# A hybrid streaming-encoder layer: the first receptance tile projected from the unscaled input, the output's row tiles finished one by one

## The chip, the cores and the metric

One core of a Trainium2 chip runs the whole kernel. The metric is the device time of one execution in microseconds (us), the median of several runs.

## The reference

One layer on a sequence of 512 tokens with 1024 channels, all in float32. `rms_norm`, one wide projection, three token mixers side by side (a short gated convolution, an RG-LRU, an RWKV-7 time mix with a state of 64 x 64 per head), a gated merge, an output projection with a residual, then a squared-ReLU MLP with a residual, and a last `rms_norm`.

```python
h = rms_norm(x, norm1_g[l])
p = h @ w_in[l]                       # 12 wide pieces, r, k, v among them
pc = token_shift(pc, rwkv_mu[l])      # p + (previous token's p - p) * mu
r, k, v, xw, xa, xg = _split(pc, ...)
...
y = rwkv7_recurrence(r, decay, k, v, kk, a)   # in chunks of 64 tokens
...
x = x + m @ w_out[l]
x = x + jnp.square(jax.nn.relu(h2 @ mlp_w1[l])) @ mlp_w2[l]
return rms_norm(x, final_g)
```

`rms_norm` divides by the root of the mean square over the channels and multiplies by a gain. The division is one number per token, so `h @ w` can be had as `(x * gain) @ w`, divided afterwards.

## The kernel before

Activations lie transposed in SBUF: channels on the 128 partitions (8 slices, `KT`), the 512 tokens along the free axis. Each float32 matrix product is made of three matmuls of a fast kind (`mm3`, lines 163 to 165): every operand is split in a high part (`whi`, `hh`) and the rest (`wlo`, `hl`). One projection tile of 128 output channels is 24 matmuls of 128x128 by 512 columns in one PSUM bank. Its weights come by one DMA on SP's queue (`raw`, two buffers); ScalarE casts the high part (`whi`, line 142) and VectorE subtracts for the low part (`wlo`, line 99), three buffers each.

In the prologue, the unscaled input times the gain is split into `xgh`, `xgl`; the first projections (`lr0`, `lr1`, and `k0`) are made of these (`proj_raw`), while the sum of squares and its inverse root `rsb` are worked out. Their results are then multiplied by `rsb` (`unscaled`) and mixed with the token before (`shift`: one ScalarE and one VectorE instruction). `pro_scale` makes `hh`, `hl` for all other projections: a multiply by `rsb` (five slices on GpSimd, three on VectorE), a ScalarE product, a VectorE difference (`hl`).

Behind it, four groups of heads run. For each, `krv` projects k, r and v of the group's channel tiles (`k0`, `r0`, `k1`, `r1`, `v0`, `v1` in group 0) and makes decay and key terms; `amat` makes the matrices `pA` of every chunk, masked into `AXt` on VectorE; `inverse` inverts a triangular matrix per chunk by substitution on VectorE (`Z`, `dg`), put together by small matmuls `pG`, `pT`; `chain` walks the chunks. `ab` is filler for TensorE: it projects the other branches (`xb`, `gb`, `gatb`, `c`, `x`, `b`, `ga`) of two channel tiles a group (tile 6 first in group 0). `weave` alternates between the critical generator and the filler; the priorities given there, and the numbers of buffers, decide the order in which each engine's instructions stand. Each engine then runs its own row strictly in that order and waits for others by semaphores.

The tail is the end of the MLP's second product. The result lies by tokens: four row tiles of 128 tokens (`i`), two halves of 512 channels each (`h`), eight PSUM banks `acc`. For the last two of 32 contraction slices, the function `last` issues the six matmuls that each half still lacks, then adds the residual, sums the squares (ScalarE, `fss`), takes the root (`fsd`), multiplies by the final gain `fgt` and scales by the inverse root. It is a generator, called in the order 0, 1, 2, 0, 1, 3, 3, 2, so that the second parts of tiles stand behind the first parts of later ones.

Of the kernel before, what the change touches and what calls it, by code (L numbers as in the profile page):

```python
# [93 lines left out]
def block_kernel(ctx, tc, xt, win, par, mulr, sw, wout, w1, w2, fg, cst, eyes, out):  # L94
# [176 lines left out]
    def proj_raw(w, t):  # L271
        for kt in range(KT):
            mm3(t, *wslice(w, kt), xgh(kt), xgl[:, kt], start=kt == 0, stop=kt == KT - 1)
# [21 lines left out]
    def shift(pt, mu, omu, o):  # L295
        ac.activation(o, pt, AF.Copy, scale=omu)
        stt(o[:, 1:], pt[:, 0:S - 1], mu, o[:, 1:], MUL, ADD)
# [32 lines left out]
    shift(unscaled(t_lr0, "us0"), mul[:, 0:1], omul[:, 0:1], lr)  # L330
    t_k0 = pp.tile([P, S], F32, tag="pp", name="pp")
    proj_raw(load_w(win[CN[("k", 0)]]), t_k0)
    ac.activation(lr[0:64], lr[0:64], AF.Tanh)
    lws = sp.tile([P, S], F32R, name="lws")
    las = sp.tile([P, S], F32R, name="las")
# [10 lines left out]
    lgh, lgl = split(sp, lg, "lg")  # L346
    k0 = WP("ks")
    shift(unscaled(t_k0, "us0"), pv("mu_k", 0), dvp(OMK, 0), k0)
    pro_ctx.close()


# [33 lines left out]
    def krv(g, G_):  # L385
        G_.AR = pk.tile([P, 2, NC, 2, L], F32, tag="AR", name="AR")
        G_.BK = pk.tile([P, 2, NC, 2, L], F32, tag="BK", name="BK")
        G_.pl = sp.tile([P, 2, NC], F32, tag="pl", name="pl", bufs=2)
        G_.v = [sp.tile([P, S], F32, tag=f"v{h}", name=f"v{h}", bufs=2) for h in range(2)]
        G_.bv = [sp.tile([P, S], F32, tag=f"bv{h}", name=f"bv{h}", bufs=2) for h in range(2)]  # L390
        for jj in range(2):
            j = 2 * g + jj
            rs = WP("rs")
            if j == 0:
                ks = k0
            else:
                ks = WP("ks")
                t = yield from proj(("k", j))
                shift(t, pv("mu_k", j), dvp(OMK, j), ks)
            sq = WP("a1")  # L400
            ac.activation(sq, ks, AF.Square, scale=pv("kk", j))
            sqh, sql = split(pk, sq, "b")
            pn = pm.tile([P, S], F32, tag="pm", name="pn")
            pe.matmul(pn, bd, sqh, start=True, stop=False)
            pe.matmul(pn, bd, sql, start=False, stop=True)
            kk = WP("a5")
            rsqrt_rows(pk, kk, pn, 1e-24)
            stt(kk, ks, pv("kk", j), kk, MUL, MUL)
            yield
            t = yield from proj(("r", j))  # L410
            shift(t, pv("mu_r", j), dvp(OMR, j), rs)
            yield
            swh, swl = load_sw(pk, "swa", j, 0, 2)
            pw = pm.tile([P, S], F32, tag="pm", name="pw")
            pe.matmul(pw, swh[:, 0], lws, start=True, stop=False)
            pe.matmul(pw, swl[:, 0], lws, start=False, stop=True)
            sig = WP("a1")
            ac.activation(sig, pw, AF.Tanh, bias=pv("w0", j), scale=0.5)
            v.tensor_scalar(out=sig, in0=sig, scalar1=1.0, scalar2=None, op0=ADD)
            pa = pm.tile([P, S], F32, tag="pm", name="pa")  # L420
            pe.matmul(pa, swh[:, 1], las, start=True, stop=False)
            pe.matmul(pa, swl[:, 1], las, start=False, stop=True)
            av = WP("a4")
            ac.activation(av, pa, AF.Tanh, bias=pv("a0", j), scale=0.5)
            cum = WP("a2")
            v.tensor_tensor_scan(out=cum, data0=smk, data1=sig, initial=0.0, op0=MUL, op1=ADD)
            PP = pk.tile([P, NC, L + 1], F32, tag="PPt", name="PPt")
            gp.memset(PP[:, :, 0:1], 1.0)
            Pt = PP[:, :, 1:L + 1]
            ac.activation(Pt, c3(cum), AF.Exp, scale=-0.5 * CW)  # L430
            v.tensor_copy(G_.pl[:, jj], PP[:, :, L])
            pinv = WP("a3")
            ac.activation(pinv, cum, AF.Exp, scale=0.5 * CW)
            stt(G_.AR[:, jj, :, 0], c3(kk), -1.0, PP[:, :, 0:L], MUL, MUL)
            tt(G_.AR[:, jj, :, 1], c3(rs), Pt, MUL)
            t_ = WP("a1")
            stt(t_, av, 1.0, kk, ADD, MUL)
            stt(G_.BK[:, jj, :, 0], c3(t_), 0.5, c3(pinv), MUL, MUL)
            kp = WP("a2")
            ts2(kp, av, pv("ka", j), dvp(OKA, j), MUL, ADD)  # L440
            tt(kp, kp, ks, MUL)
            tt(G_.BK[:, jj, :, 1], c3(kp), c3(pinv), MUL)

            if jj == 0:
                rk = [WP(f"rk{h}") for h in range(2)]
            for h in range(2):
                r = slice(64 * h, 64 * h + 64)
                stt(rk[h][64 * jj:64 * jj + 64], rs[r], part[r, PI["rk"], j:j + 1], kp[r], MUL, MUL)
        rk = [split(pk, rk[h], ("a1", "a3") if h else "b") for h in range(2)]
        for h in range(2):  # L450
            q = 2 * g + h
            t = yield from proj(("v", q))
            shift(t, pv("mu_v", q), dvp(OMV, q), G_.v[h])
            yield
        for h in range(2):
            pb = pm.tile([P, S], F32, tag="pm", name="pb")
            for i in range(2):
                pe.matmul(pb, bd, rk[h][i], start=i == 0, stop=i == 1)
            tt(G_.bv[h], pb, G_.v[h], MUL)
# [449 lines left out]
    with tc.tile_pool(name="mw", bufs=2) as mw, \  # L909
# [41 lines left out]
        with tc.tile_pool(name="fin", bufs=1, side="right") as fin:  # L951
# [19 lines left out]
                        mlp2(fi, w, i, h)  # L971
            wl2 = [load_w(w2[fi]) for fi in range(NF - 2, NF)]
            def last(i):
                ss = fin.tile([P, 2], F32, tag="fss", name="fss", bufs=2)
                x3f = xr[:, i] if i < 3 else fin.tile([P, D], F32, name="x3f")
                for h in range(2):
                    hs = slice(h * S, (h + 1) * S)
                    for d_ in range(2):
# [1 line left out]
                    stt(xr[:, i, hs], acc[i][h], sc2[:, i:i + 1], xr[:, i, hs], MUL, ADD)  # L980
                    junk = fin.tile([P, S], F32, tag="fj", name="fj", bufs=2)
                    ac.activation(junk, xr[:, i, hs], AF.Square, accum_out=ss[:, h:h + 1])
                    (v if (i, h) == (3, 0) else gp).tensor_tensor(out=x3f[:, hs], in0=xr[:, i, hs], in1=fgt[:, hs], op=MUL)
                sd = fin.tile([P, 2], F32, tag="fsd", name="fsd", bufs=2)
                tt(sd[:, 0:1], ss[:, 0:1], ss[:, 1:2], ADD)
                ac.activation(sd[:, 1:2], sd[:, 0:1], AF.Sqrt, bias=epst[:, 0:1], scale=1.0 / D)
                v.reciprocal(sd[:, 0:1], sd[:, 1:2])
                yield
                for h in range(2):
                    hs = slice(h * S, (h + 1) * S)  # L990
                    if h == 0 and i != 2:
                        ac.activation(x3f[:, hs], x3f[:, hs], AF.Copy, scale=sd[:, 0:1])
                    else:
                        v.tensor_scalar(out=x3f[:, hs], in0=x3f[:, hs], scalar1=sd[:, 0:1], scalar2=None, op0=MUL)
                    (ac if h == 0 and i != 2 else sy).dma_start(out[i, :, hs], x3f[:, hs])

            gens = [last(i) for i in range(4)]
            for i in (0, 1, 2, 0, 1, 3, 3, 2):
                next(gens[i], None)
        ps.close()  # L1000


# [72 lines left out]
```

## Time and profile before

| | us |
|---|---|
| median of 3 runs | 1125.88 |
| lowest, highest | 1125.72, 1127.33 |
| the profiled execution's own time | 1126.26 |
| its span, first to last instruction | 1124.5 |

The span is one execution as the profiler saw it; its own time is 1.76 us longer. A row of a timeline says when an instruction started, how long it took, its engine and line, what it wrote and read, and in brackets how long the engine was idle before it, and what ended that. PE is TensorE's matmul, DVE is VectorE, ACT ScalarE, POOL GpSimd, SP the queue that issues the weights' DMAs. "x2" is a run of like instructions in one row.

### The profile page before, as it was taken

The page shows a single profiled execution, that of the slowest core. Times are in us where ns is not written, and L with a number is a line of the kernel's source. Part 1 is how long each engine was busy: PE and PEld are TensorE (multiplying, and loading weights), DVE is VectorE, ACT ScalarE, POOL GpSimd, SP SyncE. Part 2 cuts the span into 40 slices and gives each one's busy share as a digit, 9 for nine tenths or more (in the row PEclk, how much of TensorE's full clock was granted, in tenths as well). Part 3 has the DMA queues.
Part 4 walks back from the last instruction along what each step waited for, and adds up shares of the span by engine and source line. Part 5 has one row for each costly group of instructions (what it writes and reads, how often), then busy time and mean ns, then how long its engine had stood idle before and what let it go on. Part 6 is the DMA issues. An engine that isn't in the chain of part 4 may idle for free.

```text
span 1124.5 us, 16256 instructions
## 1 busy us (share of the span) xinstructions
PE 1087.3 (97%) x6396; PEld 869.7 (77%) x6396; DVE 766.3 (68%) x1369; ACT 519.2 (46%) x837; POOL 58.9 (5%) x99
## 2 busy tenths in 40 slices
PE   8899989999989999989999989999999999999996
PEld 5677867778867678867678867898888888888885
DVE  7998995989986889975888967686444443222224
ACT  6655355534457534456534474564344333112113
POOL 2200000000000000000000020100000000000003
PEclk8999997999999999999999999999999999999998
DMA  6232222231233131232231262455322225322222
GB/s 212 71 103 80 73 74 77 62 103 57 90 117 99 58 103 57 89 120 88 61 95 65 85 206 85 171 180 161 109 95 94 94 94 191 105 98 94 93 94 75
DMA packets 37772, 114.60 MB, mean 102 GB/s; under 512 B 4544, under 2 KB 8128, under 8 KB 37696
## 3 DMA queue, kind: packets, MB, share of 16 engines
q1 hardware_dynamic: 30768, 95.48, 26.6%
q0 software_dynamic: 6352, 17.30, 4.5%
q8 instruction: 50, 0.82, 0.3%
q10 hardware_dynamic: 576, 0.79, 0.2%
q14 instruction: 26, 0.21, 0.1%
HBM read 104.64 MB, written 8.91 MB: 101 GB/s over the span
## 4 chain that ended last, share of the span: by engine, by line
PE 71%; DVE 22%; issue 3%; ACT 2%; DMA 1%; SPq 0%; ACTq 0%; DVEq 0%
PE pp L163 8%; PE pp L164 8%; PE pp L165 8%; PE acc L165 6%; PE acc L164 6%; PE acc L163 6%; PE p L164 5%; PE p L165 5%; PE p L163 5%; DVE wlo L99 5%; DVE dg L99 4%; DVE Z L99 3%; PE pA L471 2%; DVE u L102 2%; PE py L578 2%
## 5 line engine op out<-in xcount | busy, mean ns | idle before, releaser
L99 DVE TENSOR_TENSOR wlo<-raw,whi 128x1024 fp32r<-128x1024 f32 (+1 forms) x172 | 209.4, 1218 | 215.7 <-ACT whi L142 213.6
L142 ACT CAST whi<-raw 128x1024 fp32r<-128x1024 f32 (+1 forms) x172 | 178.1, 1036 | 286.1 <-PE acc L165 125.7
L165 PE MATMUL pp<-hh,wlo 128*128 128x512 f32 x696 | 278.0, 401 | 5.8 <-DVE wlo L99 5.8
L164 PE MATMUL pp<-hl,whi 128*128 128x512 f32 x696 | 278.3, 400 | 3.9 <-DVE hl L102 3.9
L163 PE MATMUL pp<-hh,whi 128*128 128x512 f32 x696 | 278.5, 401 | 1.4 <-DVE ks L102 0.6
L165 PEld LDWEIGHTS pp<-hh,wlo 128*128 128x128 f32 x696 | 131.9, 190 | 34.4 <-DVE wlo L99 7.3
L163 PEld LDWEIGHTS pp<-hh,whi 128*128 128x128 f32 x696 | 132.0, 190 | 31.9 <-ACT u L664 2.1
L164 PEld LDWEIGHTS pp<-hl,whi 128*128 128x128 f32 x696 | 132.0, 190 | 31.6 <-DVE hl L102 4.7
L165 PE MATMUL p<-h2h,wlo 128*128 128x512 f32 (+1 forms) x264 | 101.2, 383 | 0.0
L163 PE MATMUL p<-h2h,whi 128*128 128x512 f32 (+1 forms) x264 | 101.1, 383 | 0.0
L164 PE MATMUL p<-h2l,whi 128*128 128x512 f32 (+1 forms) x264 | 101.0, 383 | 0.0
L163 PE MATMUL acc<-whi,ah 128*128 128x512 f32 x256 | 99.6, 389 | 0.0
L164 PE MATMUL acc<-wlo,ah 128*128 128x512 f32 x256 | 99.6, 389 | 0.0
L165 PE MATMUL acc<-whi,al 128*128 128x512 f32 x256 | 99.6, 389 | 0.0
L165 PEld LDWEIGHTS p<-h2h,wlo 128*128 128x128 f32 x264 | 49.6, 188 | 9.7
L163 PEld LDWEIGHTS p<-h2h,whi 128*128 128x128 f32 x264 | 49.6, 188 | 9.7
L164 PEld LDWEIGHTS p<-h2l,whi 128*128 128x128 f32 x264 | 49.6, 188 | 9.5
L165 PEld LDWEIGHTS acc<-whi,al 128*128 128x128 f32 x256 | 48.0, 188 | 10.1
L164 PEld LDWEIGHTS acc<-wlo,ah 128*128 128x128 f32 x256 | 48.0, 188 | 10.1
L163 PEld LDWEIGHTS acc<-whi,ah 128*128 128x128 f32 x256 | 48.0, 188 | 9.8
L99 DVE TENSOR_TENSOR Z<-Z,dg 64x31 f32<-64x31 f32 (+15 forms) x124 | 42.2, 340 | 4.1
L99 DVE TENSOR_TENSOR dg<-Z 64x31 f32<-64x31 f32 (+15 forms) x124 | 42.2, 340 | 4.1
(299 smaller groups left out, 1533.8 us busy)
## 6 DMA issues: line engine op xcount, KB each, us to landing
raw<-in_win SPq DMA_DIRECT2D x88, 512.0 KB, 3.5
raw<-in_w SPq DMA_DIRECT2D x64, 512.0 KB, 3.5
raw<-in_wout SPq DMA_DIRECT2D x16, 512.0 KB, 3.5
swr<-in_sw SPq DMA_DIRECT2D x16, 128.0 KB, 2.1
x2T<-in_xt POOLq DMA_DIRECT2D x4, 512.0 KB, 7.1
x2d<-st POOLq DMA_DIRECT2D x8, 256.0 KB, 2.6
xr<-x2d POOLq DMA_DIRECT2D x1, 2048.0 KB, 9.1
xT<-in_xt SPq DMA_DIRECT2D x3, 512.0 KB, 6.7
```

What stands on the lines that cost most here:

```text
L99: return v.tensor_tensor(out=o, in0=a, in1=b, op=op)
L102: return v.scalar_tensor_tensor(out=o, in0=a, scalar=s, in1=b, op0=op0, op1=op1)
L142: ac.copy(hi[:, sl], raw[:, sl])
L163: pe.matmul(ps, wh, xh, start=start, stop=False)
L164: pe.matmul(ps, wh, xl, start=False, stop=False)
L165: pe.matmul(ps, wl, xh, start=False, stop=stop)
L471: pe.matmul(pts[h][:, ci], G_.BK[rows, jj, c], G_.AR[rows, jj, c], start=True, stop=True)
L578: mm = pe.matmul(py[64 * h:64 * h + 64, jj], w, x, start=first and jj == 0, stop=last, skip_group_check=True)
```

## The change

There are two parts. In the prologue the projection of `r0` is made by `proj_raw` from the unscaled input, into the PSUM bank of the pool's tag `pS` (which the state products use later), and is multiplied by `rsb` before its `shift`; `krv` of group 0 then takes `r0` as it takes `k0`. In the tail, `last` is a plain function that finishes one row tile after the other: the first half is multiplied by the gain on GpSimd and scaled on ScalarE, the second half gets both in one VectorE product, and the two halves go out on ScalarE's and SP's queue.

```diff
     proj_raw(load_w(win[CN[("k", 0)]]), t_k0)
+    t_r0 = pc.tile([P, S], F32, tag="pS", name="pr")
+    proj_raw(load_w(win[CN[("r", 0)]]), t_r0)
...
     shift(unscaled(t_k0, "us0"), pv("mu_k", 0), dvp(OMK, 0), k0)
+    r0 = WP("rs")
+    shift(unscaled(t_r0, "us1"), pv("mu_r", 0), dvp(OMR, 0), r0)
...
-            rs = WP("rs")
             if j == 0:
-                ks = k0
+                rs, ks = r0, k0
             else:
-                ks = WP("ks")
+                rs, ks = WP("rs"), WP("ks")
...
-            t = yield from proj(("r", j))
-            shift(t, pv("mu_r", j), dvp(OMR, j), rs)
-            yield
+            if j > 0:
+                t = yield from proj(("r", j))
+                shift(t, pv("mu_r", j), dvp(OMR, j), rs)
+                yield
...
-                x3f = xr[:, i] if i < 3 else fin.tile([P, D], F32, name="x3f")
+                sd = fin.tile([P, 2], F32, tag="fsd", name="fsd", bufs=2)
...
-                    (v if (i, h) == (3, 0) else gp).tensor_tensor(out=x3f[:, hs], in0=xr[:, i, hs], in1=fgt[:, hs], op=MUL)
-                sd = fin.tile([P, 2], F32, tag="fsd", name="fsd", bufs=2)
+                x0, x1 = xr[:, i, 0:S], xr[:, i, S:D]
+                o0 = x0 if i < 3 else fin.tile([P, S], F32, name="x3f")
+                gp.tensor_tensor(out=o0, in0=x0, in1=fgt[:, 0:S], op=MUL)
...
-                yield
-                for h in range(2):
-                    hs = slice(h * S, (h + 1) * S)
-                    if h == 0 and i != 2:
-                        ac.activation(x3f[:, hs], x3f[:, hs], AF.Copy, scale=sd[:, 0:1])
-                    else:
-                        v.tensor_scalar(out=x3f[:, hs], in0=x3f[:, hs], scalar1=sd[:, 0:1], scalar2=None, op0=MUL)
-                    (ac if h == 0 and i != 2 else sy).dma_start(out[i, :, hs], x3f[:, hs])
-
-            gens = [last(i) for i in range(4)]
-            for i in (0, 1, 2, 0, 1, 3, 3, 2):
-                next(gens[i], None)
+                stt(x1, x1, sd[:, 0:1], fgt[:, S:D], MUL, MUL)
+                sy.dma_start(out[i, :, S:D], x1)
+                ac.activation(o0, o0, AF.Copy, scale=sd[:, 0:1])
+                ac.dma_start(out[i, :, 0:S], o0)
+
+            for i in range(4):
+                last(i)
```

The first place is TensorE's row in the prologue, around the last matmul of `k0` (`pp_265` in both kernels). Before, `pp_412` is `r0` and `pp_426` is `xb6`:

```order
L165 MATMUL pp_412<-hh_73,wlo_408 128x512
L163 MATMUL pp_412<-hh_73,whi_407 128x512
L165 MATMUL pp_265<-xgh_92,wlo_268 128x512
L163 MATMUL pp_426<-hh_73,whi_421 128x512
L164 MATMUL pp_426<-hl_74,whi_421 128x512
L165 MATMUL pp_426<-hh_73,wlo_422 128x512
```

In the changed kernel `pp_487` is `k1`, and `pr_296` is the `r0` of the new code:

```order
L165 MATMUL pp_487<-hh_73,wlo_483 128x512
L163 MATMUL pp_487<-hh_73,whi_482 128x512
L165 MATMUL pp_265<-xgh_92,wlo_268 128x512
L163 MATMUL pr_296<-xgh_91,whi_298 128x512
L164 MATMUL pr_296<-xgl_93,whi_298 128x512
L165 MATMUL pr_296<-xgh_91,wlo_299 128x512
```

The rows ahead of the last `pp_265`, on `hh` and `hl`, are `k1`'s where they were `r0`'s, and the rows of the unscaled `r0` stand where `xb6`'s were.

The second place is VectorE's row before the first transpose of group 0's inverse (`Z`). Before (`u`, `g` tiles are filler, `wlo_1068` a weight of the filler):

```order
L102 SCALAR_TENSOR_TENSOR u2_825<-u5_843,u2_825 128x512
L99 TENSOR_TENSOR AXt_868<-pA_895,mask_65 128x512
L99 TENSOR_TENSOR AXt_868<-pA_896,mask_65 128x512
L99 TENSOR_TENSOR u1_472<-u1_472,u2_825 128x512
L99 TENSOR_TENSOR AXt_868<-pA_913,mask_65 128x512
L99 TENSOR_TENSOR AXt_868<-pA_914,mask_65 128x512
L710 SCALAR_TENSOR_TENSOR u5_849<-u4_834,u1_472 128x512
L102 SCALAR_TENSOR_TENSOR g2_534<-g2_534,u5_849 128x512
L99 TENSOR_TENSOR AXt_868<-pA_931,mask_65 128x512
L99 TENSOR_TENSOR AXt_868<-pA_932,mask_65 128x512
L99 TENSOR_TENSOR wlo_1068<-raw_1066,whi_1067 128x1024
L495 STREAM_TRANSPOSE Z_1016<-AXt_868 32x32x32 x2
```

In the changed kernel (`wlo_1030` is a weight whose buffer `c6` had):

```order
L99 TENSOR_TENSOR AXt_820<-pA_858,mask_65 128x512
L99 TENSOR_TENSOR AXt_820<-pA_859,mask_65 128x512
L99 TENSOR_TENSOR wlo_1030<-raw_1028,whi_1029 128x1024
L102 SCALAR_TENSOR_TENSOR u1_573<-u3_886,u1_573 128x512
L99 TENSOR_TENSOR swbl_1269<-swr_1266,swbh_1268 128x256
L99 TENSOR_TENSOR AXt_820<-pA_907,mask_65 128x512
L99 TENSOR_TENSOR AXt_820<-pA_908,mask_65 128x512
L499 STREAM_TRANSPOSE Z_998<-AXt_820 32x32x32 x2
L99 TENSOR_TENSOR u3_892<-u3_892,g2_595 128x512
L99 TENSOR_TENSOR dg_999<-Z_998 64x31
L99 TENSOR_TENSOR swcl_2198<-swr_2195,swch_2197 128x128
```

The filler products that stood between the `AXt` rows, the scan of line 710 among them, now come behind the transpose, and a weight's `wlo` stands ahead of the last two `AXt`.

The third place is the end of VectorE's row. Before, from the sum of squares of tile 2 (`fsd_9530`) on:

```order
L102 SCALAR_TENSOR_TENSOR xr2_8535<-acc_8545,sc2_8527,xr2_8535 128x512
L99 TENSOR_TENSOR fsd_9530<-fss_9509 128x1
L983 TENSOR_TENSOR x3f_9543<-xr2_8535,fgt_8537 128x512
L987 RECIPROCAL fsd_9530<-fsd_9530 128x1
L102 SCALAR_TENSOR_TENSOR xr2_8535<-acc_8546,sc2_8527,xr2_8535 128x512
L994 TENSOR_SCALAR xr2_8535<-xr2_8535,fsd_9530 128x512
...
L99 TENSOR_TENSOR fsd_9564<-fss_9542 128x1
L987 RECIPROCAL fsd_9564<-fsd_9564 128x1
L994 TENSOR_SCALAR x3f_9543<-x3f_9543,fsd_9564 128x512
```

(The scaling of line 994 is there twice, for both halves of tile 2.) In the changed kernel:

```order
L102 SCALAR_TENSOR_TENSOR xr2_8537<-xr2_8537,fsd_9490,fgt_8539 128x512
L99 TENSOR_TENSOR fsd_9518<-fss_9517 128x1
L102 SCALAR_TENSOR_TENSOR xr2_8537<-acc_8548,sc2_8529,xr2_8537 128x512
L993 RECIPROCAL fsd_9518<-fsd_9518 128x1
L102 SCALAR_TENSOR_TENSOR xr2_8537<-xr2_8537,fsd_9518,fgt_8539 128x512
L99 TENSOR_TENSOR fsd_9546<-fss_9545 128x1
L993 RECIPROCAL fsd_9546<-fsd_9546 128x1
L102 SCALAR_TENSOR_TENSOR xr2_8537<-xr2_8537,fsd_9546,fgt_8539 128x512
```

The last product of an accumulator (`acc_8548` after, `acc_8546` before) no longer has the product into `x3f` ahead of it, but the fused product of tile 1 (`fsd_9490`); the scalings behind it are gone, and one fused product takes their place.

## Rows read from the trace of the kernel before

**Rows 1.** The page: the span, and each engine's busy time and instructions.

```profile
span 1124.5 us, 16256 instructions
PE 1087.3 (97%) x6396; PEld 869.7 (77%) x6396; DVE 766.3 (68%) x1369; ACT 519.2 (46%) x837; POOL 58.9 (5%) x99
```

**Rows 2.** Timeline of VectorE and TensorE, prologue and start of group 0.

```profile
25.90 0.69 DVE L99 TENSOR_TENSOR us<-pp,rsb 128x512 f32<-128x512 f32 x1
31.67 3.44 DVE L102 SCALAR_TENSOR_TENSOR hl<-xT,n1t,hh 128x512 fp32r<-128x512 f32 x2
35.63 0.74 DVE L102 SCALAR_TENSOR_TENSOR hl<-xT,n1t,hh 128x512 fp32r<-128x512 f32 x1
...
33.48 0.50 PE L164 MATMUL pp<-hl,whi 128*128 128x512 f32 x1 [3.16 <-DVE hl L102]
...
42.32 0.39 PE L163 MATMUL pp<-hh,whi 128*128 128x512 f32 x1
...
43.45 0.39 PE L163 MATMUL pp<-hh,whi 128*128 128x512 f32 x1
...
67.18 0.74 DVE L102 SCALAR_TENSOR_TENSOR ks<-pp,part,ks 128x511 f32<-128x511 f32 x1
```

**Rows 3.** Windows: busy time of each engine, then the granted clock (PEclk).

```profile
core 0: us, PE busy (x) PEld busy (x) DVE busy (x) ACT busy (x) POOL busy (x), PEclk, DMA share, GB/s
35.00:38.50 3.50, 3.34 (x8) 2.66 (x9) 3.50 (x7) 2.68 (x4) 0.00 (x0) 0.52 0.02 5
168.10:181.70 13.60, 12.40 (x111) 9.35 (x111) 3.76 (x8) 7.33 (x14) 0.54 (x1) 0.50 0.31 97
320.00:324.00 4.00, 3.77 (x17) 3.06 (x17) 3.23 (x4) 3.29 (x6) 0.00 (x0) 1.00 0.49 155
488.00:492.00 4.00, 3.77 (x10) 2.74 (x11) 3.18 (x4) 3.24 (x5) 0.00 (x0) 0.64 0.46 150
```

**Rows 4.** Timeline of VectorE and TensorE, the inverse of group 0.

```profile
108.76 4.18 DVE L495 STREAM_TRANSPOSE Z<-AXt 32x1024 f32<-32x1024 f32 x2
...
152.67 4.26 DVE L512 STREAM_TRANSPOSE Z<-Z 32x1024 f32<-32x1024 f32 x2
...
169.30 3.62 PE L530 MATMUL pT<-Z,dg 32*32 32x32 f32 x64 [4.78 <-ACT dg L524]
```

**Rows 5.** Timeline of the tail: TensorE, VectorE, GpSimd, ScalarE.

```profile
1114.60 0.39 PE L165 MATMUL acc<-whi,al 128*128 128x512 f32 x1
...
1115.64 0.80 DVE L99 TENSOR_TENSOR fsd<-fss 128x1 f32<-128x1 f32 x1
...
1117.04 0.73 DVE L102 SCALAR_TENSOR_TENSOR xr<-acc,sc,xr 128x512 f32<-128x512 f32 x1
1117.69 1.88 DVE L994 TENSOR_SCALAR xr<-xr,fsd 128x512 f32<-128x512 f32 x2
...
1115.16 1.26 POOL L983 TENSOR_TENSOR xr<-xr,fgt 128x512 f32<-128x512 f32 x1 [0.40 <-ACT fj L982]
...
1119.67 0.29 ACT L986 ACTIVATE fsd<-fsd,epst 128x1 f32<-128x1 f32 x1 [1.06 <-DVE fsd L99]
1120.20 0.72 ACT L992 ACTIVATE x3f<-x3f,fsd 128x512 f32<-128x512 f32 x1 [0.23 <-DVE fsd L987]
```

**Rows 6.** Groups of VectorE, 90 to 110: busy, mean ns | idle before, releaser.

```profile
L99 DVE TENSOR_TENSOR wlo<-raw,whi 128x1024 fp32r<-128x1024 f32 x2 | 2.4, 1222 | 2.2 <-ACT whi L142 2.2
...
L102 DVE SCALAR_TENSOR_TENSOR u<-u,u 128x512 f32<-128x512 f32 x2 | 1.4, 692 | 0.8 <-ACT u L692 0.4 <-ACT u L704 0.3
...
L710 DVE TENSOR_TENSOR_SCAN u<-u,u 128x512 f32<-128x512 f32 x1 | 1.2, 1215 | 0.0
...
L99 DVE TENSOR_TENSOR u<-u,g 128x512 f32<-128x512 f32 x1 | 0.7, 692 | 0.7 <-ACT u L699 0.7
L99 DVE TENSOR_TENSOR u<-u,u 128x512 f32<-128x512 f32 x1 | 0.7, 692 | 0.2 <-POOL u L707 0.2
...
L99 DVE TENSOR_TENSOR swcl<-swr,swch 128x128 fp32r<-128x128 f32 x1 | 0.3, 293 | 0.1
```

**Rows 7.** Timeline of TensorE, the first matrices of group 0.

```profile
95.96 1.49 PE L471 MATMUL pA<-AR,BK 64*128 64x128 f32 x16
```

**Rows 8.** Groups of ScalarE, 40 to 100 us.

```profile
L142 ACT CAST whi<-raw 128x1024 fp32r<-128x1024 f32 x10 | 10.5, 1048 | 16.3 <-PE pp L164 16.3
```

**Rows 9.** TensorE's waits over the span: us in total, times, longest.

```profile
PE pga L163 <- ACT uh L158: 4.9, 2, 2.5
```

## The prediction

> **What bounds the kernel now.** I read the page first: TensorE is busy 97% of the span, VectorE 68% [rows 1]. Then I looked for the places where TensorE is idle, because only there, at the half clock and behind the last matmul can this change gain or lose: it has the same matmuls before and after. Two such places lie where the change works. In the prologue TensorE waits 3.16 us at 33.48 for the first `hl` tiles, which VectorE makes late [rows 2], and the granted clock then falls to half for a while (0.52 in 35.0 to 38.5, [rows 3]). At 169.30 it waits 4.78 us for the inverse of group 0, and from 168.1 to 181.7 the clock is 0.50 [rows 3, 4]. That inverse is VectorE's: a transpose that starts at 108.76, a substitution, and a transpose that ends at 152.67 + 4.26 = 156.93 [rows 4]. The last place is the tail, behind the last matmul at about 1115: a chain of VectorE, ScalarE and a DMA up to 1124.5 [rows 1, 5].
>
> The sum is made against the profiled execution: span 1124.5, own time 1126.26, 0.4 above the median of 1125.88. A measurement can tell about 0.2%, 2.25 us, from no change.
>
> **The prologue.** The diff reads as if `r0`'s 24 matmuls, which need no scaled input, would fill the 3.16 us. The order of the instructions says otherwise: TensorE's queue still has matmuls on `hh` and `hl` in that place, `k1`'s now where `r0`'s stood, and `r0`'s come only behind the last of `k0`, where `xb6`'s stood. So the wait, VectorE's rows that make `hl`, and the fall of the clock stay. In SP's queue `k1`'s weights take the place of `xb6`'s behind `r0`'s; no transfer is added. The part that is added is one multiply by `rsb`, 0.69 us by the multiply of the same kind at 25.90 [rows 2]; VectorE is nearly full until 108, so it counts there.
>
> **What really moves.** With `r0` out of its generator, `k1`, `r1`, `v0`, `v1` of group 0 run ahead of the filler projections (`xb6`, `gb6`, `gatb6`, `c6`), and the matrices `pA` come earlier in TensorE's row. By the time TensorE reaches `pG`, both kernels have issued the same matmuls. What counts is when VectorE starts and ends the inverse.
>
> Gains: VectorE's waits in 90 to 110 were for filler work, 2.2 + 0.8 + 0.7 + 0.2 = 3.9 us [rows 6]. That filler now stands behind the start of the inverse, so these waits go.
>
> New waits: (a) `k1`'s shift writes the one `ks` buffer, which is free only when `k0`'s last reader is done; VectorE's part of that shift ends at 67.18 + 0.74 = 67.9 now [rows 2], and its place in VectorE's row hardly changes, so the square and the cast behind it give TensorE its operand at about 69. TensorE, 108 rows on from 42.32 at 0.226 a row (42.32 to 43.45 is five, [rows 2]), is there at about 67: 1.7 us of wait, and I count 0.6, 0.8 and 0.75 more for `bl`, for `pb` and for `pA`'s two banks, estimates of the same kind; 3.85 in all. (b) `wlo_1030` now stands ahead of the last two `AXt` products on VectorE; its weight buffer is free only with `c6`'s last matmul. From 42.32, 223 matmuls of 0.226 are 50.4, 32 of `pA` at 1.49 / 16 are 3.0 [rows 7], and with the 3.85 that is 99.6. The cast takes 1.05 [rows 8], `wlo` 1.22 [rows 6], and one product, one small `swbl` and two `AXt` of 0.68 each follow, 2.4 together: the transpose of the inverse can start at about 104.3, 4.5 us earlier than 108.76, though VectorE will have waited about as long at `wlo_1030`.
>
> What is given back: a `wlo` (1.22), the scan (1.22) and six smaller products (0.3 to 0.69) that stood before the inverse now lie inside it, less one that leaves it; 5.0 us at their pitch [rows 6]. So it ends at 104.3 + 48.2 + 5.0 = 157.5, where it ended at 156.93: +0.5. Behind it ScalarE's row (the product's tanh, table loads, casts, the copies of `AXt` and `dg`) is unchanged and starts as much later; walked row by row it came out up to 1.7 later at `pT`. I take **+1.0**. Bounds: if the four waits under (a) do not appear, `c6` ends 3.85 earlier and `pT` comes 2.9 earlier; if they are twice as long, it comes 4.8 later. TensorE is idle before `pT` in any case, so its own 3.85 costs only what reaches VectorE through (b). From `pT` on, the order on all engines is that of before, so the shift stays to the end.
>
> **The tail.** Now: VectorE's `fsd` sum of the third row tile, 128 numbers, takes 0.80 and ends as GpSimd's multiply does (1115.16 + 1.26 = 1116.42), and with the multiply into `x3f` behind it the last product of the accumulators starts at 1117.04, two us after the last matmul; then two scalings, 1.88 us, stand before the last `fsd`; `Sqrt` at 1119.67, the reciprocal, and the last scale 1120.20 to 1120.92 [rows 5]; the span ends 3.6 later, with the transfer. After: four multiplies on GpSimd in place of seven, none of them the last step, and one fused product per row tile in place of the scalings. If the fused products run at 0.74 beside GpSimd, the last accumulator product starts at 1115.8; then 0.74, square and its read 0.8, a scale 0.72 now ahead of the last `Sqrt`, 0.3, reciprocal 0.2, and 0.72: the last issue is at 1119.4, 1.5 earlier. If they wait out GpSimd's multiplies, it starts at 1117.2 and ends at 1120.8, 0.1 earlier. What speaks for waiting: `hl`, of this form, took 1.72 beside GpSimd's multiplies and 0.74 alone [rows 2], and `fsd` waits to their end. I take **-0.9**; bounds 0 and -2.0 (no wait, and the transfers spread out).
>
> The Trainium skill (GPSIMD Engine Reference, Key points) says that GpSimd contends for SBUF with VectorE's instructions that have two SBUF inputs. The rows for `hl` and `fsd` agree, and the fused product is such an instruction while the scaling that it replaces is not; by the rule alone the tail would gain 0.1.
>
> **The sum.** +1.0 - 0.9 = +0.1 on the profiled time; against the median I forecast 1126.0 us.
>
> **The rivals.**
> (1) No change by these two terms, 0.45: 1126.0, itself between 1123.7 and 1128.1.
> (2) Slower, 0.28: the waits at `wlo_1030` are longer than I count. It needs TensorE to reach `c6`'s end after 101.8; each us later there is a us at `pT`. The two waits of 1.7 and 0.6 lie 1 us apart, and a clock fall behind them would do it: two waits for `pga`, 4.9 together with 2.5 the longest [rows 9], were followed once by clock 1.00 (320 to 324) and once by 0.64 (488 to 492) [rows 3]. A stretch like that of 35.0 to 38.5 at half speed costs 1.7. With that, and `ks` late by 1.5, `pT` comes 4.2 later and the tail gains 0.5: 1129.6.
> (3) Faster, 0.20: the waits (a) are covered by filler rows, `pT` is 2.9 earlier, the tail gains 1.5: 1121.5. Or TensorE, reaching `pT` later than before by its own waits, idles 2.6 us there in place of 4.8, and the clock stays up: of the 13.6 us at 0.50, half is at stake, but the small matmuls of `pT` and the chain's first steps do not fill TensorE, so I expect little of it.
> (4) The change does what the code's order suggests, 0.07: `r0` fills the 3.16 us and the half clock behind it (1.7) goes too, 4.9 less and the tail: 1120.1. Against it stands TensorE's row order, which the queue cannot change; for it only that weights or `hl` might arrive otherwise.
>
> Faster is (3) and (4), 0.27; same 0.45; slower 0.28. The range 1122.3 to 1129.6 takes in (2) and part of (3), and leaves out (4) and the ends of both bounds.
>
> **What would show it.** The wait for `hl` at 33 to 34 and a low clock behind it remain. A new TensorE wait of 1 to 2 us near 67, for `bh`. VectorE idle some us before `wlo` near 96 to 100; the transpose of the inverse at 104 to 105, its end at 157 to 159; `pT` between 169 and 172, and the last matmul later by the same. In the tail the last accumulator product starts 0.8 to 2.2 us behind the last matmul's end (1114.99, [rows 5]), and the last scale ends 4.4 to 5.8 us behind it, where it is 5.9 now. I am wrong if `pT` moves by over 2.5 us, or if there are more or fewer stretches at half clock.

## The result, and the profile after

The changed kernel takes 1130.65 us in the median of six executions (1128.44 to 1131.86), the kernel before 1125.8 in six (1125.35 to 1127.33): a ratio of 1.004, 95% interval [1.003, 1.0051]. It is slower by 0.4%, and 1.05 us above the upper end of the range.

The execution that was profiled is the fastest of the six (1128.44). The page answers to [rows 1]:

```profile
span 1126.7 us, 16252 instructions
PE 1088.4 (97%) x6396; PEld 870.6 (77%) x6396; DVE 764.3 (68%) x1368; ACT 519.0 (46%) x838; POOL 55.1 (5%) x96
```

Busy times are those of before within 4 us, with as many matmuls; so the loss must lie in when things happen. The timeline of TensorE, as in [rows 2, 4, 5], at the four places of the forecast:

```profile
32.44 0.80 PE L164 MATMUL pp<-hl,whi 128*128 128x512 f32 x1 [3.16 <-DVE hl L102]
...
62.95 0.50 PE L163 MATMUL pp<-hh,whi 128*128 128x512 f32 x1 [2.17 <-DVE rs L102]
...
172.88 3.62 PE L534 MATMUL pT<-Z,dg 32*32 32x32 f32 x64 [5.98 <-ACT dg L528]
...
1117.91 0.39 PE L165 MATMUL acc<-whi,al 128*128 128x512 f32 x1
```

The wait for `hl` is there as it was, 3.16 us. A new wait of 2.17 us stands at 62.95: `r1`'s projection has filled its PSUM bank, and the tile behind it needs the bank before VectorE's `rs` has read it. `pT` starts at 172.88 where it started at 169.30, and the last matmul comes 3.3 later. The part after `pT` is as long as before: 945.0 from the start of `pT` to that of the last matmul, 945.3 before. The time is lost ahead of `pT`. The timeline of VectorE there, to be read beside [rows 4, 6]:

```profile
95.91 0.69 DVE L99 TENSOR_TENSOR AXt<-pA,mask 128x512 f32<-128x512 f32 x1 [0.83 <-PE pA L475]
...
101.16 1.23 DVE L99 TENSOR_TENSOR wlo<-raw,whi 128x1024 fp32r<-128x1024 f32 x1 [4.55 <-ACT whi L142]
102.81 0.69 DVE L102 SCALAR_TENSOR_TENSOR u<-u,u 128x512 f32<-128x512 f32 x1 [0.42 <-ACT u L696]
103.80 0.42 DVE L99 TENSOR_TENSOR swbl<-swr,swbh 128x256 fp32r<-128x256 f32 x1 [0.30 <-PE pA L475]
...
105.46 4.13 DVE L499 STREAM_TRANSPOSE Z<-AXt 32x1024 f32<-32x1024 f32 x2
...
155.01 4.23 DVE L516 STREAM_TRANSPOSE Z<-Z 32x1024 f32<-32x1024 f32 x2
159.27 0.69 DVE L102 SCALAR_TENSOR_TENSOR u<-u,u 128x512 f32<-128x512 f32 x1
...
161.33 0.69 DVE L99 TENSOR_TENSOR u<-u,g 128x512 f32<-128x512 f32 x1 [0.22 <-ACT u L703]
162.26 1.23 DVE L99 TENSOR_TENSOR wlo<-raw,whi 128x1024 fp32r<-128x1024 f32 x1 [0.24 <-ACT whi L142]
```

The inverse starts at 105.46, earlier than 108.76, but ends at 155.01 + 4.23 = 159.24, later than 156.93. The groups of VectorE within the inverse, 105.46 to 159.22, show what it now does inside:

```profile
L99 DVE TENSOR_TENSOR wlo<-raw,whi 128x1024 fp32r<-128x1024 f32 x7 | 8.6, 1226 | 0.2
...
L714 DVE TENSOR_TENSOR_SCAN u<-u,u 128x512 f32<-128x512 f32 x1 | 1.2, 1225 | 0.0
...
L99 DVE TENSOR_TENSOR u<-u,u 128x512 f32<-128x512 f32 x1 | 0.7, 692 | 0.0
L102 DVE SCALAR_TENSOR_TENSOR g<-g,u 128x512 f32<-128x512 f32 x1 | 0.7, 692 | 0.0
...
L99 DVE TENSOR_TENSOR u<-u,g 128x512 f32<-128x512 f32 x1 | 0.7, 691 | 0.0
L102 DVE SCALAR_TENSOR_TENSOR g<-u,u 128x512 f32<-128x512 f32 x1 | 0.7, 691 | 0.0
L99 DVE TENSOR_TENSOR swcl<-swr,swch 128x128 fp32r<-128x128 f32 x1 | 0.3, 292 | 0.0
```

Within the inverse of before there are six `wlo`, and none of the other six groups; all its other groups are the same, and the substitution itself (31 products `Z` and 31 `dg`, 21.1 us) is as long. What is added is 1.23 + 1.23 + 4 x 0.69 + 0.29 = 5.5 us of filler between the steps.

Windows of the granted clock (last but two in a row; columns as in [rows 3]):

```profile
31.50:38.30 6.80, 5.83 (x13) 4.16 (x14) 6.77 (x9) 3.67 (x6) 2.01 (x2) 0.52 0.08 30
171.40:181.60 10.20, 8.72 (x86) 6.75 (x88) 3.03 (x4) 5.78 (x11) 0.54 (x1) 0.51 0.38 129
321.00:326.00 5.00, 4.47 (x12) 3.37 (x13) 3.74 (x4) 4.43 (x7) 0.00 (x0) 0.66 0.58 171
```

The stretch behind the `hl` wait is 6.8 us long at the lower of the two levels, where it was 3.4; the one at `pT` is 10.2 where it was 13.6; near 321, where the clock stayed at 1.00, there is now a short one.

The tail gained. VectorE, GpSimd and ScalarE, beside [rows 5]:

```profile
1117.84 1.87 DVE L102 SCALAR_TENSOR_TENSOR xr<-xr,fsd,fgt 128x512 f32<-128x512 f32 x1
1119.63 0.15 DVE L99 TENSOR_TENSOR fsd<-fss 128x1 f32<-128x1 f32 x1
1119.70 0.74 DVE L102 SCALAR_TENSOR_TENSOR xr<-acc,sc,xr 128x512 f32<-128x512 f32 x1
...
1120.54 0.75 DVE L102 SCALAR_TENSOR_TENSOR xr<-xr,fsd,fgt 128x512 f32<-128x512 f32 x1
...
1117.88 1.28 POOL L990 TENSOR_TENSOR x3f<-xr,fgt 128x512 f32<-128x512 f32 x1
...
1122.28 0.72 ACT L996 ACTIVATE x3f<-x3f,fsd 128x512 f32<-128x512 f32 x1 [0.29 <-DVE fsd L993]
```

The last scale ends 1122.28 + 0.72 - (1117.91 + 0.39) = 4.70 behind the last matmul's end, where it was 5.93.

### The profile page after: what moved, and what is told of

Its sections match the earlier page's. It is cut to its first block, busy times and chain, and to the rows that moved or that the text cites. A ratio compares the mean times of both kernels' runs of the same rounds, so it can differ in the third digit from the quotient of the medians.

```text
span 1126.7 us, 16252 instructions
## 1 busy us (share of the span) xinstructions
PE 1088.4 (97%) x6396; PEld 870.6 (77%) x6396; DVE 764.3 (68%) x1368; ACT 519.0 (46%) x838; POOL 55.1 (5%) x96
## 3 DMA queue, kind: packets, MB, share of 16 engines
q10 hardware_dynamic: 720, 1.05, 0.3%
## 4 chain that ended last, share of the span: by engine, by line
PE 76%; DVE 18%; issue 3%; ACT 2%; DMA 1%; SPq 0%; ACTq 0%; DVEq 0%
PE pp L163 10%; PE pp L165 9%; PE pp L164 9%; PE acc L164 6%; PE acc L165 6%; PE acc L163 6%; PE p L165 5%; PE p L163 5%; PE p L164 5%; DVE wlo L99 4%; DVE dg L99 3%; DVE Z L99 3%; PE pA L475 2%; DVE u L102 2%; PE py L582 2%
## 5 line engine op out<-in xcount | busy, mean ns | idle before, releaser
L165 PE MATMUL pp<-hh,wlo 128*128 128x512 f32 x688 | 274.9, 400 | 5.8 <-DVE wlo L99 5.8
L163 PE MATMUL pp<-hh,whi 128*128 128x512 f32 x688 | 275.5, 402 | 3.1 <-DVE rs L102 2.2
L164 PE MATMUL pp<-hl,whi 128*128 128x512 f32 x688 | 274.8, 399 | 3.2 <-DVE hl L102 3.2
L163 PE MATMUL p<-h2h,whi 128*128 128x512 f32 (+1 forms) x264 | 101.1, 383 | 0.0
```

What stands on the lines that cost most here:

```text
L163: pe.matmul(ps, wh, xh, start=start, stop=False)
L164: pe.matmul(ps, wh, xl, start=False, stop=False)
L165: pe.matmul(ps, wl, xh, start=False, stop=stop)
```

## The experiments

The question was which half of the change loses the time, and by what. There were two theories. **Pace:** `weave` takes a number of filler steps per step of the critical generator. With `r0` gone from it, `krv` of group 0 has 17 steps in place of 21; at the unchanged 0.852 they carry 14.5 filler steps in place of 17.9, and what is not issued ahead of the inverse comes to lie inside it. (The ratio of the next stage, `amat` and `inverse`, is worked out from 21 x 0.852 in every kernel here, so it is the same in all.) **r0's place:** the extra multiply, and the matmuls of `r0` in another place of TensorE's row, make the head late. The rival to both was clock stretches.

Profiles differ by up to 2 us in when `rsb` is ready (24.1 to 26.1), also where the code is the same up to the tail, as in the last two rows of the table (26.11 and 24.29). So every profile is cut from there. Before and after:

```profile
25.15 0.71 DVE L191 STREAM_TRANSPOSE rsb<-rqq 128x512 f32<-128x512 f32 x1
```
```profile
24.11 0.71 DVE L191 STREAM_TRANSPOSE rsb<-rqq 128x512 f32<-128x512 f32 x1
```

All numbers are us:

| kernel | `rsb` transpose to first `Z` | first `Z` to its end | end to `pT` | `rsb` to `pT` | tail | median | ratio to before [95%] |
|---|---|---|---|---|---|---|---|
| before | 83.61 | 48.17 | 12.37 | 144.15 | 5.93 | 1125.8 | |
| after | 81.35 | 53.78 | 13.64 | 148.77 | 4.70 | 1130.65 | 1.004 [1.003, 1.0051] |
| prologue half alone | 81.06 | 53.78 | 13.63 | 148.47 | 5.92 | 1130.62 | 1.0048 [1.0033, 1.0063] |
| tail half alone | 84.22 | 48.15 | 12.37 | 144.74 | 4.69 | 1125.56 | 0.9997 [0.9985, 1.0009] |
| change, pace 1.053 | 84.92 | 48.15 | 12.37 | 145.44 | 4.69 | 1126.79 | 1.0009 [0.9997, 1.002] |
| change, `k0` and `r0` ahead | 83.89 | 53.77 | 13.64 | 151.30 | 4.70 | 1130.4 | 1.0051 [1.0034, 1.0067] |
| before, pace 0.69 | 79.96 | 53.76 | 13.64 | 147.36 | 5.92 | 1128.9 | 1.002 [1.001, 1.0031] |
| change, pace 1.053, early `us1` | 82.11 | 48.15 | 12.37 | 142.63 | 4.71 | 1122.66 | 0.9974 [0.9956, 0.9991] |
| tail half, early `us1` | 83.30 | 48.14 | 12.37 | 143.81 | 4.71 | 1121.64 | 0.9965 [0.9952, 0.9978] |
| change, early `us1` | 80.21 | 53.78 | 13.64 | 147.63 | 4.65 | 1130.09 | 1.0044 [1.0028, 1.006] |
| change, pace 1.6, early `us1` | 79.93 | 48.65 | 13.63 | 142.21 | 4.71 | 1121.36 | 0.9964 [0.9952, 0.9976] |
| the same, last gain on VectorE | 79.93 | 48.59 | 13.64 | 142.16 | 4.07 | 1122.11 | 0.9966 [0.9955, 0.9976] |

"Tail" is from the end of the last matmul to the end of the last scale on ScalarE. The medians of before that the ratios stand against were 1126.06 for the first four experiments, 1126.37 for the next three, 1125.3 for the two behind them, 1125.58 for the last; each group ran on a chip of its own, with before beside it. Three pairs of rows have the same code up to the tail (before and the tail half, after and the prologue half, the last two): `rsb` to `pT` agrees to 0.59, 0.30 and 0.05 in them. A difference of half a us in that column is within what one profile of each can tell.

**The prologue half alone.** The changed prologue, and `last` and its calls as before:

```diff
+    t_r0 = pc.tile([P, S], F32, tag="pS", name="pr")
+    proj_raw(load_w(win[CN[("r", 0)]]), t_r0)
...
             gens = [last(i) for i in range(4)]
             for i in (0, 1, 2, 0, 1, 3, 3, 2):
                 next(gens[i], None)
...
```

> The prologue half of the change alone; the tail is that of before. Theory A (the loss is in group 0: with r0 out of its generator, the key/receptance/value work runs ahead of the filler, and filler work of VectorE lands inside the inverse): the loss of the whole change plus what its tail gains, 1126 + 4.6 + 1 = about 1131.5, and pT at 172 to 174. Rival C (the loss is the tail's, whose profile happened to be a good one): about 1126, pT near 170.

It measured 1.0048, as the whole change. The whole loss is this half's. Its low clock behind the `hl` wait was the short one, and yet the inverse started at the same distance from `rsb` (81.06 against 81.35); so the longer stretch in the profile after did not make the inverse late.

**The tail half alone.** The prologue as before, `last` as changed:

```diff
...
+            for i in range(4):
+                last(i)
```

> The tail half alone; the prologue is that of before. Theory A: faster than before by the 1.2 us that the tail of the changed kernel is shorter from the last matmul to the last scale, about 1124.6, with pT at 169.3 as before. Rival C: slower than before, 1128 or more.

It measured 0.9997 [0.9985, 1.0009]. The profile shows the 1.24 us (5.93 to 4.69), but twelve executions of it spread from 1123.1 to 1127.7, and the median does not resolve a gain of 0.1%.

**The pace restored.** 17 steps at 1.053 carry the 17.9 filler steps that 21 carried at 0.852:

```diff
-    weave(krv(0, GS[0]), AB[0], R0)
+    weave(krv(0, GS[0]), AB[0], 1.053)
```

> The whole change, with one number more changed: the filler steps per step of krv in group 0 go from 0.852 to 1.053, so that its 17 steps carry as many filler steps as the 21 of before. TensorE's and VectorE's rows then have the filler where before had it (pga, pgi and x ahead of pA). Theory A: the inverse starts and pT comes within 1 us of before (the added multiply by rsb is 0.7), the tail's gain stays: about 1125. Rival B (the loss is in r0's own new place: its bank, its multiply, k1 ahead of it): the loss stays, 1129 or more, pT at 172 or later.

The loss is gone: 1.0009 [0.9997, 1.002], and the inverse is 48.15 long again, with 12.37 behind it. `pT` comes 0.7 to 1.3 later than in the two kernels without the new `r0` (145.44 against 144.74 and 144.15), of which the added multiply is 0.68; the tail's gain does not show, and the median stays above the 1125 expected. VectorE and TensorE in this kernel:

```profile
109.12 4.18 DVE L499 STREAM_TRANSPOSE Z<-AXt 32x1024 f32<-32x1024 f32 x2
...
153.01 4.26 DVE L516 STREAM_TRANSPOSE Z<-Z 32x1024 f32<-32x1024 f32 x2
```
```profile
41.48 0.77 PE L163 MATMUL pp<-hh,whi 128*128 128x512 f32 x1 [5.23 <-DVE us L99]
...
169.64 3.62 PE L534 MATMUL pT<-Z,dg 32*32 32x32 f32 x64 [4.75 <-ACT dg L528]
```

The wait for `hl` is gone too, since `r0` now does run there, but TensorE waits 5.23 us at 41.48 for VectorE's `us`, the multiply that empties `lr1`'s PSUM bank: it ends at 41.3, behind all `hl` rows. That is a new wait in the old one's place. It also means that this run moved `r0`'s matmuls in TensorE's row, not the filler alone, so it does not part the two theories; the next one does.

**The pace alone lowered, in the kernel before.** 21 steps at 0.69 carry the 14.5 of the change; `r0` stays where it was:

```diff
-    weave(krv(0, GS[0]), AB[0], R0)
+    weave(krv(0, GS[0]), AB[0], 0.69)
```

> The kernel before, nothing of the change in it, with one number changed: 0.69 filler steps per step of krv in group 0 in place of 0.852, so that its 21 steps carry as many filler steps (14.5) as the 17 of the changed kernel. VectorE's row then has a wlo ahead of the last two AXt and the filler's products inside the inverse, as after the change. Theory A (pace): slower by the same 4 to 5 us, about 1130, pT at 172 to 173 and a VectorE wait of over 4 us at that wlo. Rival B (r0's new place): as before, about 1126, pT near 169.5 to 171.

1.002 [1.001, 1.0031]. The inverse is 53.76 long with 13.64 behind it, those of the change to 0.02, without any part of it:

```profile
101.50 1.23 DVE L99 TENSOR_TENSOR wlo<-raw,whi 128x1024 fp32r<-128x1024 f32 x1 [4.34 <-ACT whi L142]
...
105.80 4.11 DVE L495 STREAM_TRANSPOSE Z<-AXt 32x1024 f32<-32x1024 f32 x2
...
155.34 4.22 DVE L512 STREAM_TRANSPOSE Z<-Z 32x1024 f32<-32x1024 f32 x2
```

So the pace accounts for 147.36 - 144.15 = 3.2 us of the 4.6 at `pT`; the inverse starts 3.65 earlier and pays 5.6 and 1.3 for it. The other 1.1 to 1.4 (81.06 and 81.35 against 79.96) are lost before the inverse, and need `r0` in its new place. The median says less: it is 2.5 us slower than before, where 4 to 5 were expected and the prologue half lost 4.6. Pace is shown to lengthen the inverse; of the lost time, it alone makes a half (by the median) to two thirds (at `pT`).

**`k0` and `r0` put ahead.** If the `hl` wait could be filled, is it worth it? The unscaled matmuls of both get a priority 200 ahead of their place:

```diff
-    proj_raw(load_w(win[CN[("k", 0)]]), t_k0)
...
-    proj_raw(load_w(win[CN[("r", 0)]]), t_r0)
+    with tc.high_priority(offset=200):
+        proj_raw(load_w(win[CN[("k", 0)]]), t_k0)
+        proj_raw(load_w(win[CN[("r", 0)]]), t_r0)
```

> The whole change, with k0's and r0's unscaled projections given a higher priority, so that both stand ahead of TensorE's first matmul on hl, and lr1's behind k1's. It tests the rival that r0 could fill the 3.16 us before hl. If r0's place is what matters there: the wait for hl falls under 1 us and the half clock behind it goes, 3 to 5 us earlier at the start of group 0. Theory A says that pT moves by less than that, since the order inside group 0 stays as in the changed kernel: 1126 to 1129. If the start is what counts: 1125 or less.

It is not: 1.0051 [1.0034, 1.0067], and `pT` comes 151.30 behind `rsb`, 2.5 later than in the changed kernel, although the wait for `hl` fell to 0.78 and the clock stays at 1.00 from 26 to 60. `r0`'s matmuls now wait 3.13 us themselves, at 31.21, for their `wlo` from VectorE, and the bank of `lr1` costs 1.33 at 37.82. VectorE makes all of it, and it is busy without a break from 26 to 40.

**`lr1`'s bank emptied early.** The multiply on which TensorE waited 5.23 us is moved ahead of the `xT` and `hl` rows (`OFFS` is the kernel's own offset for work that is to come early); the pace is 1.053:

```diff
+    with tc.high_priority(offset=OFFS):
+        u_lr1 = unscaled(t_lr1, "us1")
...
-    shift(unscaled(t_lr1, "us1"), mul[:, 1:2], omul[:, 1:2], lg)
+    shift(u_lr1, mul[:, 1:2], omul[:, 1:2], lg)
...
-    weave(krv(0, GS[0]), AB[0], R0)
+    weave(krv(0, GS[0]), AB[0], 1.053)
```

> The kernel with the change and the restored pace, and with the multiply of lr1's result by rsb put ahead of the hl rows on VectorE, so that its PSUM bank is free when TensorE has done r0: TensorE waited 5.23 us for it there. If that wait sets the start of group 0: the wait falls to 1 or 2 us, the half clock behind it goes, pT comes 3 to 5 us earlier, about 1122. If VectorE is the bound from 26 to 108 whatever TensorE does: the wait goes or moves, pT stays within 1 us, 1126 to 1127.

0.9974 [0.9956, 0.9991], the first that is faster than both kernels. `pT` comes 2.8 us earlier than with the pace alone. TensorE's 5.23 is now three waits, 0.70, 1.50 and 1.20, and the clock stays at 1.00 from 26 to 56, with no low stretch behind them.

**The same early multiply without `r0`'s new place**, in the kernel with the tail half alone:

```diff
+    with tc.high_priority(offset=OFFS):
+        u_lr1 = unscaled(t_lr1, "us1")
...
-    shift(unscaled(t_lr1, "us1"), mul[:, 1:2], omul[:, 1:2], lg)
+    shift(u_lr1, mul[:, 1:2], omul[:, 1:2], lg)
```

> The kernel before with the new tail and with lr1's multiply by rsb put early, r0 in its generator as before. It tells what the early multiply is worth without r0's new place. If VectorE is the bound: as the new tail alone, 1125 to 1126. If TensorE's wait for hl is: no gain either, since r0 and xb6 still need hl, 1125 to 1126.5; a gain of over 2 us would mean that the bank of lr1 held TensorE before the change too.

0.9965 [0.9952, 0.9978]. The expectation read a gain of over 2 us as a sign that `lr1`'s bank held TensorE before the change too. The gain came, but the profile of before has no such wait: from 25 to 110 TensorE waits there only for `hh`, `hl` and `ks`, 4.8 in all. So the gain isn't `r0`'s: with it `pT` is 1.2 earlier (142.63 against 143.81), but the medians do not tell the two apart. Nor is it all in the chain: against the tail half alone `pT` gains 0.93, the median 3.9. The mean granted clock of all executions of each kernel shows where the rest may be: 0.985 for before, 0.9852 for the tail half alone, 0.989 here. The two profiles do not show it: from `pT` to the last matmul they take 942.5 and 942.7. What in the early multiply keeps the clock up I did not find.

**The early multiply with the change as it is**, at 0.852:

```diff
+    with tc.high_priority(offset=OFFS):
+        u_lr1 = unscaled(t_lr1, "us1")
...
-    shift(unscaled(t_lr1, "us1"), mul[:, 1:2], omul[:, 1:2], lg)
+    shift(u_lr1, mul[:, 1:2], omul[:, 1:2], lg)
```

> The changed kernel with its own pace (0.852), and only the early multiply of lr1's result. It tells whether the early multiply alone makes up for the loss. From the runs so far: the part of the inverse that is longer by 5.6 us and the 1.3 us behind it belong to the order that the pace makes, so they stay (53.8 and 13.6 us); the start of the inverse comes 1 to 2 us earlier. About 1128, slower than before by 1 to 2.5. If the early multiply cures the loss: 1124 or less, with 48.2 and 12.4.

1.0044 [1.0028, 1.006]: it cures nothing there. `pT` comes 1.1 earlier than in the changed kernel (147.63 against 148.77), as expected, but the median stays at 1130 where 1128 was expected, and the mean granted clock is 0.985, that of before; so the early multiply does not by itself keep the clock up. TensorE waits 2.33 us for `hh` and 1.48 for `hl` where it waited 3.16, 1.90 for `r1`'s bank, and the inverse is 53.78 long again.

**More pace**, 1.6 in the kernel with early `us1`:

```diff
-    weave(krv(0, GS[0]), AB[0], 1.053)
+    weave(krv(0, GS[0]), AB[0], 1.6)
```

> The kernel with the change, the early multiply, and a still higher pace, 1.6 filler steps per step in place of 1.053: the filler goes further ahead of the inverse's matrices. If the length of the inverse depends on which filler products stand inside it: 48.2 or less, but a later start, since VectorE does more before it; pT about as in the run with 1.053 or up to 2 us later, 1122 to 1125. If more pace is simply better: under 1121.

0.9964 [0.9952, 0.9976], 1121.36 us, the lowest median of all, and faster than both kernels; it isn't told apart from the kernel with the new tail and early `us1` but no new `r0`. The later start that was expected did not come: the inverse starts as early as with too little pace (79.93), but is 48.65 long. Inside it are a seventh `wlo` and one small product less than before; the scan and the other products are done ahead of it. The part behind it stays at 13.63. TensorE at `pT`, in this kernel and in the next one, which is the same up to the tail:

```profile
168.32 2.34 PE L536 MATMUL pT<-Z,dg 32*32 32x32 f32 x64 [3.35 <-ACT dg L530]
```
```profile
166.45 3.62 PE L536 MATMUL pT<-Z,dg 32*32 32x32 f32 x64 [3.29 <-ACT dg L530]
```

The wait is 3.3 us in both, in place of 4.78. The 64 small matmuls took 2.34 in one, where the granted clock is 0.92 over 168.3 to 170.6, and 3.62 as before in the other, where it is 0.50 for all of them; so the shorter wait does not of itself keep the clock up there.

**The last gain on VectorE**, to take GpSimd's multiply from beside the fused product:

```diff
-                gp.tensor_tensor(out=o0, in0=x0, in1=fgt[:, 0:S], op=MUL)
+                (gp if i < 3 else v).tensor_tensor(out=o0, in0=x0, in1=fgt[:, 0:S], op=MUL)
```

> The kernel of the run with 1.6 filler steps, and in the tail the last multiply of GpSimd (into x3f) on VectorE. In the changed kernel VectorE's fused product of the second row tile took 1.87 beside that multiply, where the other three took 0.75. If GpSimd's multiply is what held it: 0.75 for all four, or little more, and the last scale ends 4.2 to 4.4 us behind the last matmul in place of 4.7. If it was something else (ScalarE, the PSUM reads): one product of 1.9 stays, and the tail is 0.7 longer by the added multiply, 5.4. The total moves by less than can be measured, about 1121.

The fused product that took 1.87 in the changed kernel, and 1.88 with pace 1.6, takes 0.74, with 0.71 for the multiply that VectorE now makes itself:

```profile
1111.97 0.71 DVE L992 TENSOR_TENSOR x3f<-xr,fgt 128x512 f32<-128x512 f32 x1
1112.61 0.74 DVE L102 SCALAR_TENSOR_TENSOR xr<-xr,fsd,fgt 128x512 f32<-128x512 f32 x1
```

The tail goes from 4.71 to 4.07, somewhat further than the 4.2 expected. The median, 0.9966 [0.9955, 0.9976], doesn't resolve 0.6 us.

## Why the prediction was wrong

The forecast was 1126.0 with no measurable change as the likeliest; it came out slower. The step that failed is the head term, "I take +1.0". It measured +4.6 (148.77 - 144.15). That filler moves into the inverse was seen, but each of the term's three parts came out worse than forecast. Two of the prediction's own signs of being wrong came true as well: `pT` moved by more than 2.5 us, and there is a stretch at the lower clock near 321 that was not there. The three parts:

- **The start of the inverse**, "about 104.3, 4.5 us earlier". It came 2.3 earlier counted from `rsb` (81.35 against 83.61). Of the 2.2 that are missing, 1.5 is a wrong count: "32 of `pA` at 1.49 / 16 are 3.0". TensorE made 48 before `c6`'s end; the groups of TensorE between 41.3 and 100.1 show it:

```profile
L475 PE MATMUL pA<-AR,BK 64*128 64x128 f32 x48 | 5.5, 285 | 0.0
```

The rows of the order said so: of the four pairs of `AXt`, only the last stood behind `wlo_1030`, so three times 16 `pA` lay ahead. At my own 1.49 a group that puts `c6`'s end at 101.1; in the time base of before it measured 100.08 + 1.04 = 101.12 (`rsb` came 1.04 earlier), since ScalarE's cast into the freed buffer starts at 100.08:

```profile
100.08 1.05 ACT L142 CAST whi<-raw 128x1024 fp32r<-128x1024 f32 x1 [8.80 <-PE pp L164]
```

That the sum then meets the time to 0.02 is luck. Of the 3.85 us of waits under (a) only 2.17 + 0.64 = 2.81 came, and the 48 `pA`, which stand in four runs between other matmuls, were busy for 5.5 us where 1.49 a group makes 4.5; the two errors of 1.0 cancel. The other 0.7 are the two waits behind `wlo_1030` (0.42 and 0.30), which I had let go with the 3.9 us. `wlo_1030`'s own wait was 4.55, as the forecast's "about as long" had it.
- **Inside the inverse**, "5.0 us": 53.78 - 48.17 = 5.6. What moved inside is what I had counted: a `wlo`, the scan and five smaller products, six less one. I had priced them at their pitch; their full lengths make 5.5, and the inverse grew by that and 0.1.
- **Behind it**, +0.5 taken: 1.27. The rows of before to compare with those from 159.27 on:

```profile
156.96 0.69 DVE L99 TENSOR_TENSOR u<-u,g 128x512 f32<-128x512 f32 x1
157.57 1.23 DVE L517 STREAM_TRANSPOSE dg<-Z 32x1024 f32<-32x1024 f32 x1
158.73 1.17 DVE L99 TENSOR_TENSOR wlo<-raw,whi 128x1024 fp32r<-128x1024 f32 x1
```

The product at 159.27, which stood before the inverse, has taken the place ahead of `dg`'s transpose that `u<-u,g` had (156.96). That one now comes behind the transpose, at 161.33, and it and the `wlo` behind it wait 0.22 and 0.24 for ScalarE: from the end of the inverse to this `wlo` it is 3.02 in place of 1.80, and all behind it is later by as much. My walk along the rows gave 1.7 at `pT`, 1.2 more than at the end of the inverse; I took less than it gave.

Together the three parts miss by 2.2 + 0.6 + 0.8 = 3.6, the distance from +1.0 to +4.6. Rival 2 had the right place, `wlo_1030`, and said that each us there is a us at `pT`; `c6`'s end came 0.7 short of the 101.8 that it asked for, and it named the clock and `ks` for what was a count. The bound given for the head, "4.8 later", would have put the time at 1126.0 + 3.8 = 1129.8; the range ended just below it.

What I did not see at all is that most of this is a matter of one number, the filler steps per critical step. I had written that filler "now stands behind the start of the inverse, so these waits go" under gains. It is most of the loss: 5.6 us inside and 1.3 behind, for 3.65 in front (the kernel before with the lower pace).

The other steps:

- **The prologue**, "the wait, VectorE's rows that make `hl`, and the fall of the clock stay": right, 3.16 us in both. That rival 4, `r0` filling the wait, would give nothing even where `r0` runs there is shown by the kernel with the pace restored (5.23 at `lr1`'s bank in its place) and by the one with `k0` and `r0` ahead. This holds as long as the bank is emptied late; with the early multiply, `r0` in the gap goes with a `pT` 1.2 earlier.
- **New waits of TensorE (a):** 1.7 near 67 for `bh` was wrong in place and cause; it was 2.17 at 62.95 for `r1`'s PSUM bank, which `rs` frees. `bl` cost 0.6, as counted; the 0.8 and 0.75 for `pb` and `pA`'s banks did not come.
- **The tail**, -0.9: -1.23, right and somewhat small. The last accumulator product started 1.40 behind the last matmul's end (forecast 0.8 to 2.2). Of my two cases it was the one with waiting: the fused product ahead of it took 1.87 in place of 0.74, 1.13 more beside a multiply of 1.28, and ended 0.55 behind that multiply. It came out less than forecast because the multiply ended 0.86 behind the last matmul, where I had 1.43 (1116.42 - 1114.99), and the product 0.55 behind it, where I had 0.74. By the Trainium skill's rule alone (GPSIMD Engine Reference, Key points: GpSimd contends with VectorE's instructions of two SBUF inputs) the tail would have gained 0.1. The rule holds here, 1.87 beside GpSimd's multiply and 0.74 without it, but three of the four fused products do not meet a multiply of GpSimd.
- **The clock.** Behind `pT` both profiles hold 20.5 us at the lower level; the mean granted clock over all executions is 0.9858 after (six) and 0.985 before (23). The loss is not the clock's.

What stays open is which part of `r0`'s new place (0.69 for its multiply, the late bank) makes the 1.1 to 1.4 that the pace does not explain; and why the medians differ by 4.85 where the measured terms, +4.6 and -1.2, make 3.4. The profiled execution, the fastest of its kernel, cannot tell; the prologue half alone, profiled at 1130.78, close to its median, has 1.0 more between `pT` and the last matmul than before.

## What to carry to other kernels

When a step leaves a generator that is woven with filler by a fixed ratio, the filler thins out with it: count the steps times the ratio before and after, and set the ratio anew. Then count what the scheduler has moved from in front of a serial section into it, since that is paid in full where an earlier start is not: here 5.5 us of products moved, the section grew by 5.6, and its start gained 3.65 at most. And before a wait is filled with other work, look at which bank or buffer that work needs next and who frees it: here the engine that made the wait also had to free the bank.

## What was not expected of the hardware

- A VectorE product of two SBUF operands and a scalar, 128x512, took 1.87 us beside a GpSimd multiply of 1.28, ending 0.55 behind it, and 0.74 without; an accumulator product at 1116.98, with one operand in PSUM, took 0.75 beside such a multiply; the sum of 128 numbers in the tail fell from 0.80 to 0.15 when no multiply of GpSimd lay beside it.
- Executions of one kernel on one chip spread over 2 to 8 us (before: 1122.45 to 1128.08 in 23). Part of it goes with the clock: over all 70 executions of before behind the experiments, the 34 with a mean granted clock of 0.985 or less took 1126.8 on average, the other 36 took 1125.0. The low stretches differ between profiles too: behind a wait for `pga` near 320 us the clock stayed at 1.00 in one and fell (0.66 over 321 to 326) in the other, and it fell near 320 in the tail half alone too, whose code up to there is that of before. A gain of 1.2 us that every profile shows cannot be seen in a median here.
